# Two mixed pairs of single panels in another order, and a logarithm given out in three steps, in a one-layer hybrid inference step

## The chip, the cores and the metric

The kernel runs on one core of a Trainium2 chip. The metric is the device time of one execution in microseconds (us). Three runs of the kernel before took 1439.19, 1437.35 and 1439.19 us, median 1439.19.

## What is computed

One layer of a hybrid encoder, for 1024 prompt tokens and 64 sample tokens (T = 1088 rows, D = 1024), in float32. Cut to what matters here:

```python
xn = rms_norm(x, g_pre)
z = xn @ w_in
xa, ga, q, k, v, gb, fl, ma, mb = split(z)
logf = log_sigmoid(fl + b_f)
cum = cumsum(logf)
yb = fox_attend(q, k, v, cum, cum) * silu(gb)
log_a = -LRU_C * r * softplus(-a_param)
ya = rg_lru(causal_conv(xa), log_a) * silu(ga)
mix = sum(sigmoid([ma, mb]) * [ya @ w_a, yb @ w_b]) @ w_o
h = x + rms_norm(mix, g_post)
```

Both `log_sigmoid` and `softplus` go through one helper, `half_log1p_exp_neg_abs`: an exponential on ScalarE, and on VectorE a reciprocal and a series in seven coefficients. The keys, the values and `logf` are outputs too.

## The kernel before, in words

Every float32 product is made of three products of rounded halves: a high part (copied to fp32r by ScalarE, `copy_act`, L84) and the rest (subtracted by VectorE or GpSimd, `sub`, L87) of each operand, xh·wh, xh·wl and xl·wh. So each panel of weights that is loaded has to be split before TensorE can take it.

The stage of this change is the projection to keys, queries and some gates, from about 150 to 423 us of the span. It takes two panels of 128 columns at a time, a quad: `quads` (L224 to L230) lists twelve, numbered 0 to 11. Quads 0 to 7 are pairs of neighbouring panels of keys and queries by turns; quads 8 and 9 are mixed: two single panels each, out of the x path of branch A (`d_x0`, kind "r") and its gates (`d_ga`, kind "g"); 10 and 11 are pairs of merge or branch gates. `seven` (L852 on) makes a quad by seven products of halves, as in Strassen's scheme, with three PSUM banks (`ta`, `tb`, `tcc`), each used by two products or three. I call the n-th product of quad i qi.n. Each is 24 matmuls of 128x272 (`product`, L785 to L794). After q.1 ScalarE copies `ta` to `p1`, and q.3 adds on into `ta`, so it waits for that copy. After q.2 VectorE makes `u2` = `tb` + `p1` (L880), and q.4 adds on into `tb`, so it waits for `u2`. After q.4 VectorE makes `u3` (L897), and q.6 waits for that. The quarters of the result go through `put` (L817 on): a "k" or "q" quarter is split again (`oh` on ScalarE, `kl`, or for queries in place `ko`, on VectorE), and both parts are sent to DRAM, the `oh` by ScalarE's queue and the rest by SP's queue. A "g" quarter passes a Sigmoid on ScalarE (L827) and a product on VectorE (L828), an "r" quarter is sent as it is. `load_pair` (L623 on, its DMAs at L247) loads the panels of quad i + 2 at the start of quad i; `split_pair` splits those of quad i + 1 while quad i runs: GpSimd makes the four sums of panel halves (`s1`, `s2`, `s4`), ScalarE and VectorE the splits `wh` and `wl`.

Beside the quads runs a chain of small work, the generator `running_sums` (L700 to L767). `between`, called after every product, takes the chain one step on after every third product. Its steps, in this order:

- the forget gate's logarithm (`ls_e`, `ls_s`, `ls_q`, 128x144; the row of six at L158 is the series), `fl` (L710), `lf` (L711) and two DMAs that send `logf`;
- two steps with nothing in them;
- five matmuls for the cumulative sums (L720 to L724), and on VectorE `off` (L728 to L730) and `cs` (L732, L733);
- one step with nothing in it, and then eight steps, for each a transpose `ct` (L738), the six rows `cr` (L741 to L744, two of them casts on GpSimd) and a DMA to `d_rows`;
- two transposes `cs_t` (L748, L749), `cs_h` and `cs_n` (L753 to L755), and their DMAs;
- the softplus of the recurrence's parameter (`sp_e`, `sp_s`, `sp_q`, 128x8, with L764 to L767 behind it): seventeen instructions on VectorE and one exponential on ScalarE.

TensorE executes in the order in which the program is written. On ScalarE, VectorE, GpSimd and SP a scheduler sets the order in this stage, from the written order and its own costs; so a yield that is put into the chain doesn't by itself decide where the instructions behind it come to stand. A DMA takes one of eight lanes in turn and waits for the DMA that had its lane eight before.

Of the kernel before, what the change touches and what calls it, by code (L numbers as in the profile page):

```python
# [13 lines left out]
P = 128  # L14
D = 1024
KT = D // P
# [11 lines left out]
C_XA, C_GA, C_Q, C_K, C_V, C_GB, C_FL, C_MA, C_MB = (  # L28
    0, 1024, 2048, 3072, 4096, 5120, 6144, 6160, 7184)
# [20 lines left out]
GA_EARLY = (1, 3, 5)  # L50
LN1P = [1.0 / 15, 1.0 / 13, 1.0 / 11, 1.0 / 9, 1.0 / 7, 1.0 / 5, 1.0 / 3]
# [16 lines left out]
def hybrid_step(tc, a, o):  # L68
    nc = tc.nc
    PSUM = bass.MemoryType.PSUM  # L70
    act, dve, pool, pe, sp = nc.scalar, nc.vector, nc.gpsimd, nc.tensor, nc.sync

    def sb(name, bufs=1, side=None):
        kw = {"side": side} if side else {}
        return Pool(tc, name=name, bufs=bufs, reuse_waits="tile", **kw)
# [4 lines left out]
    def f(ap):  # L80
        return ap.bitcast(F32)

    def copy_act(out, in_, scale=1.0):
        return act.activation(out=out, in_=in_, func=AF.Copy, scale=scale)  # L84

    def sub(eng, out, in0, in1):
        return eng.tensor_tensor(out=out, in0=in0, in1=in1, op=ALU.subtract)  # L87
# [10 lines left out]
    d_ga = dram.tile([KT, P, T], F32, name="d_ga")  # L98
    d_x0 = dram.tile([P, T], F32, name="d_x0")
# [28 lines left out]
    def tiny(n, name, w=1, tag=None):  # L128
        return small.tile([P, w], F32, name=name, tag=tag or name)[:n, :]
# [17 lines left out]
    def half_log1p_exp_neg_abs(pl, x, w, name):  # L147

        e, s, q = (pl.tile([P, w], F32, name=f"{name}_{k}")[:, :] for k in "esq")
        tc.keep_in_program_order(dve.scalar_tensor_tensor(out=e, in0=x, scalar=-1.0, in1=x, op0=ALU.mult, op1=ALU.max))  # L150
        act.activation(out=e, in_=e, func=AF.Exp, scale=-1.0)
        dve.tensor_scalar(out=s, in0=e, scalar1=2.0, scalar2=None, op0=ALU.add)
        dve.reciprocal(out=s, in_=s)
        dve.tensor_tensor(out=s, in0=s, in1=e, op=ALU.mult)
        dve.tensor_tensor(out=q, in0=s, in1=s, op=ALU.mult)
        dve.tensor_scalar(out=e, in0=q, scalar1=LN1P[0], scalar2=None, op0=ALU.mult)
        for c in LN1P[1:]:
            dve.scalar_tensor_tensor(out=e, in0=e, scalar=c, in1=q, op0=ALU.add, op1=ALU.mult)  # L158
        dve.scalar_tensor_tensor(out=e, in0=e, scalar=1.0, in1=s, op0=ALU.add, op1=ALU.mult)
        return e  # L160
# [57 lines left out]
    def cols(c, n=2):  # L218
        return w_in[:, c:c + n * P]
# [2 lines left out]
                  for k in range(0, KT, 2))  # L222

    quads = [([cols(c + p * P)], ((t, p), (t, p + 1))) for p in range(0, NP, 2) for c, t in ((C_K, "k"), (C_Q, "q"))]  # L224
    some = [(cols(C_XA, 1), d_x0)] + [(cols(C_GA + k * P, 1), d_ga[k]) for k in GA_EARLY]
    for (s1, d1), (s2, d2) in (some[:2], some[2:]):
        quads.append(([s1, s2], (("r" if d1 is d_x0 else "g", d1), ("g", d2))))
    for _ in range(MORE):
        src, (d1, d2) = gates.pop()
        quads.append(([src], (("r", d1), ("r", d2))))  # L230
# [450 lines left out]
    p1b = sb("p1b")  # L681
# [18 lines left out]
    def running_sums():  # L700
        tri = p1b.tile([P, P], F32, name="tri")
        pool.memset(tri[:, :], 1.0)
        pool.affine_select(out=tri[:, :], in_=tri[:, :], compare_op=ALU.is_ge, fill=0.0,
                           base=0, pattern=[[1, P]], channel_multiplier=-1)
        nfl = (NBLK + 1) * NH
        fl2 = fl.rearrange("p b h -> p (b h)")
        hl = half_log1p_exp_neg_abs(p1b, fl2, nfl, "ls")
        lf = p1b.tile([P, NBLK + 1, NH], F32, name="lf")
        lf2 = lf.rearrange("p b h -> p (b h)")
        tc.keep_in_program_order(dve.tensor_scalar(out=fl2, in0=fl2, scalar1=0.0, scalar2=None, op0=ALU.min))  # L710
        dve.scalar_tensor_tensor(out=lf2, in0=hl, scalar=-2.0, in1=fl2, op0=ALU.mult, op1=ALU.add)  # L711
        sp.dma_start(o["logf_prompt"].rearrange("(b p) h -> p b h", p=P), lf[:, :NBLK, :])
        sp.dma_start(o["logf_sample"], lf[:DEC, NBLK, :])
        yield
        yield
        yield
        nb = NBLK * NH
        s_p = mm.tile([P, 512], F32, name="cum_p", tag="acc")
        cum_p, tot_p, cs_p, cs_p2 = s_p[:, :nb], s_p[:, nb:2 * nb], s_p[:, 2 * nb:2 * nb + NH], s_p[:, 2 * nb + NH:][:, :NH]
        pe.matmul(cum_p, tri[:, :], lf2[:, :nb], start=True, stop=True)  # L720
        pe.matmul(tot_p, ones[:, :P], lf2[:, :nb], start=True, stop=True)
        pe.matmul(cs_p, tri[:, :], lp[:, :], start=True, stop=True)
        pe.matmul(cs_p2[:DEC, :], ones[:, :DEC], lp[:, :], start=True, stop=False)
        pe.matmul(cs_p2[:DEC, :], tri[:DEC, :DEC], lf[:DEC, NBLK, :], start=False, stop=True)  # L724
        off = p1b.tile([P, NBLK, NH], F32, name="off")
        dve.memset(off[:, 0, :], 0.0)
        for b in range(1, NBLK):
            dve.tensor_tensor(out=off[:, b, :], in0=tot_p[:, (b - 1) * NH:b * NH], in1=off[:, b - 1, :], op=ALU.add)  # L728
        off2 = off.rearrange("p b h -> p (b h)")
        dve.tensor_tensor(out=off2, in0=cum_p, in1=off2, op=ALU.add)  # L730
        cs = p1b.tile([P, 2, NH], F32, name="cs")
        dve.tensor_copy(cs[:, 0, :], cs_p)  # L732
        dve.tensor_copy(cs[:DEC, 1, :], cs_p2[:DEC, :])  # L733
        yield
        yield
        for b in range(NBLK):
            ct = mm.tile([P, 512], F32, name="ct", tag="acc")[:NH, :P]
            pe.transpose(ct, off[:, b, :], ident[:, :])  # L738
            cr = p1b.tile([NH, 6, P], F32R, name="cr", tag="cr", bufs=1)
            copy_act(cr[:, 4, :], ct)  # L740
            sub(dve, cr[:, 5, :], ct, f(cr[:, 4, :]))  # L741
            dve.tensor_scalar(out=cr[:, 0:2, :], in0=f(cr[:, 4:6, :]), scalar1=-1.0, scalar2=None, op0=ALU.mult)
            for j in (2, 3):
                pool.tensor_copy(cr[:, j, :], ones[:NH, :P])  # L744
            sp.dma_start(d_rows[:, :, b * P:(b + 1) * P], f(cr[:, :, :]))
            yield
        cs_t = mm.tile([P, 512], F32, name="cs_t", tag="acc")
        pe.transpose(cs_t[:NH, :PAST], cs[:, 0, :], ident[:, :])  # L748
        pe.transpose(cs_t[:NH, PAST:PAST + DEC], cs[:DEC, 1, :], ident[:DEC, :DEC])  # L749
        cs_h = p1b.tile([NH, 2, PAST + DEC], F32R, name="cs_h")  # L750
        cs_n = p1b.tile([NH, 2, PAST + DEC], F32, name="cs_n")
        cs_t = cs_t[:NH, :PAST + DEC]
        copy_act(cs_h[:, 0, :], cs_t)  # L753
        sub(dve, cs_h[:, 1, :], cs_t, f(cs_h[:, 0, :]))
        dve.tensor_scalar(out=cs_n[:, :, :], in0=f(cs_h[:, :, :]), scalar1=-1.0, scalar2=None, op0=ALU.mult)  # L755
        sp.dma_start(d_cs, cs_n[:, :, :])
        sp.dma_start(d_cq.rearrange("s h t -> h s t"), f(cs_h[:, :, PAST:]))
        yield

        ap_ = vt[:, V_AP:V_AP + KT]  # L760
        hl2 = half_log1p_exp_neg_abs(p1b, ap_, KT, "sp")
        neg = p1b.tile([P, KT], F32, name="neg")
        tc.keep_in_program_order(
            dve.tensor_scalar(out=neg[:, :], in0=ap_, scalar1=-1.0, scalar2=0.0, op0=ALU.mult, op1=ALU.max))  # L764
        dve.scalar_tensor_tensor(out=neg[:, :], in0=hl2, scalar=2.0, in1=neg[:, :], op0=ALU.mult, op1=ALU.add)
        dve.tensor_scalar(out=sp4[:, :], in0=neg[:, :], scalar1=4.0, scalar2=None, op0=ALU.mult)
        dve.tensor_scalar(out=nsp8[:, :], in0=neg[:, :], scalar1=-8.0, scalar2=None, op0=ALU.mult)  # L767

    chain = running_sums()
    owed = deque()
    n_prod = [0]
# [1070 lines left out]
    for of in range(KT):  # L1845
        g = g_next
# [57 lines left out]
    for of in range(KT):  # L1904
        g, ma_ = m_next
# [244 lines left out]
    ss, r = tiny(n, "ss"), tiny(n, "r_r")  # L2150
    dve.tensor_reduce(out=ss, in_=ss4[:n, :], axis=AX.X, op=ALU.add)
    rstd_of(ss, r, 1.0 / D)
    for i in range(2):
        c = slice(i * D // 2, (i + 1) * D // 2)
# [52 lines left out]
```

## Time and profile before

| | |
|---|---|
| runs | 1439.19, 1437.35, 1439.19 us (median 1439.19) |
| the profiled execution | 1441.83 us; its span 1440.1 us |
| TensorE (PE) busy | 1417.7 us, 98% of the span |
| VectorE (DVE), ScalarE (ACT), GpSimd (POOL) | 851.2, 714.4, 276.9 us |
| chain that ended last | 89% PE, 5% DMA, 3% DVE, 1% ACT |

The span is one profiled execution; what lies around it (1.73 us here) is outside of its records. In the views, a row of a timeline begins with the start and the duration in us, and in brackets stands how long the engine was idle before it and what ended the wait. L793 is the matmul of the products of halves, L84 and L87 are the two helpers of the splits. SPq and ACTq rows are the issues of DMAs, not their transfers.

### The profile page before, as it was taken

What the parts mean: (1) busy time and instruction counts of PE and PEld (TensorE: products, weight loads), DVE (VectorE), ACT (ScalarE), POOL (GpSimd) and SP (SyncE); (2) the same over time, 40 slices, a digit from 0 to 9 for tenths busy, and PEclk for the clock granted to TensorE, in tenths of its full rate; (3) what the DMA queues carried; (4) which work ended last, traced back from release to release, by engine and by line L of the source; (5) the groups of instructions that cost most, each with busy time, mean ns of one, the idle gap of its engine ahead of it and who ended that gap; (6) DMA issues with size and microseconds to landing.
All of it is one profiled execution on the core that took longest, in us unless ns stands there. A gap on an engine that the chain in (4) does not pass through costs nothing.

```text
span 1440.1 us, 23751 instructions
## 1 busy us (share of the span) xinstructions
PE 1417.7 (98%) x8925; PEld 1352.0 (94%) x8925; DVE 851.2 (59%) x1495; ACT 714.4 (50%) x1297; POOL 276.9 (19%) x362
## 2 busy tenths in 40 slices
PE   8999999999999999999999999999999999999997
PEld 8999999989999999999999999999999999888886
DVE  5563855565524666565666657798755454337644
ACT  4423444334315666566666648878643322325543
POOL 0003324232313323333332320010023000000000
PEclk9999999999999999999999999999999999999999
DMA  5357456664368474545646354232296534224111
GB/s 204 115 131 106 133 156 189 140 173 137 84 174 218 127 154 127 143 122 147 132 117 154 61 95 58 45 57 47 102 299 212 188 126 151 74 70 166 48 48 45
DMA packets 134126, 182.68 MB, mean 127 GB/s; under 512 B 22276, under 2 KB 98604, under 8 KB 134012
## 3 DMA queue, kind: packets, MB, share of 16 engines
q1 hardware_dynamic: 116028, 154.90, 42.5%
q10 hardware_dynamic: 17680, 25.64, 5.0%
q8 instruction: 70, 1.15, 0.3%
q0 software_dynamic: 304, 0.62, 0.1%
q14 instruction: 44, 0.36, 0.1%
HBM read 122.65 MB, written 58.46 MB: 126 GB/s over the span
## 4 chain that ended last, share of the span: by engine, by line
PE 89%; DMA 5%; DVE 3%; ACT 1%; issue 1%; SPq 1%; ACTq 0%; DVEq 0%; POOL 0%; POOLq 0%
PE acc L165 16%; PE acc L166 16%; PE acc L167 16%; PE quad L793 15%; PE tp L1151 4%; PE pv L1179 2%; PE pv L1177 2%; PE s L1131 2%; PE s L1130 2%; PE vacc L458 1%; DMA w_raw<-in_w_in 1%; DMA d_q<-ko 1%; PE vacc L165 1%; DMA wf_raw<-in_w_in 1%; PE vacc L166 1%
## 5 line engine op out<-in xcount | busy, mean ns | idle before, releaser
L165 PE MATMUL acc<-xh,wh 128*128 128x368 f32 (+1 forms) x768 | 255.7, 333 | 0.0
L166 PE MATMUL acc<-xl,wh 128*128 128x368 f32 (+1 forms) x768 | 251.4, 327 | 0.0
L167 PE MATMUL acc<-xh,wl 128*128 128x368 f32 (+1 forms) x768 | 251.0, 327 | 0.0
L166 PEld LDWEIGHTS acc<-xl,wh 128*128 128x128 f32 x768 | 144.6, 188 | 3.1
L165 PEld LDWEIGHTS acc<-xh,wh 128*128 128x128 f32 x768 | 144.4, 188 | 3.0
L167 PEld LDWEIGHTS acc<-xh,wl 128*128 128x128 f32 x768 | 144.5, 188 | 0.0
L87 DVE TENSOR_TENSOR tl<-tp,th 128x512 fp32r<-128x512 f32 (+1 forms) x160 | 100.0, 633 | 57.9 <-ACT th L84 57.5
L84 ACT ACTIVATE th<-tp 128x512 fp32r<-128x512 f32 (+1 forms) x160 | 87.0, 552 | 66.4 <-PE tp L1151 59.7
L87 DVE TENSOR_TENSOR wl<-w_raw,wh 128x1024 fp32r<-128x1024 f32 (+1 forms) x65 | 74.1, 1140 | 58.6 <-ACT wh L84 49.5
L84 ACT ACTIVATE wh<-w_raw 128x1024 fp32r<-128x1024 f32 (+1 forms) x65 | 63.2, 974 | 72.5 <-PE acc L166 29.3
L1116 POOL TENSOR_SCALAR pb<-pb,sm 128x640 f32<-128x640 f32 (+1 forms) x64 | 61.8, 966 | 150.1 <-DVE sm L1115 150.1
L793 PE MATMUL quad<-xh,wh 128*128 128x272 f32 x384 | 81.9, 295 | 3.5 <-ACT p__3338 L84 3.5
L793 PE MATMUL quad<-xl,wh 128*128 128x272 f32 x384 | 80.5, 291 | 0.0
L793 PE MATMUL quad<-xh,wl 128*128 128x272 f32 x384 | 80.3, 291 | 0.0
L1113 ACT ACTIVATE pb<-pb,nm 128x640 f32<-128x640 f32 (+1 forms) x64 | 63.2, 987 | 25.3 <-DVE nm L1110 24.4
L1177 PE MATMUL pv<-tl,vv 128*128 128x512 f32 x192 | 74.4, 390 | 0.0
L1130 PE MATMUL s<-k,q 128*128 128x128 f32 (+2 forms) x192 | 66.9, 353 | 0.0
L1110 DVE CUSTOM_DVE_ANT_0 pb<-s,mask 128x640 f32<-128x640 f32 (+1 forms) x64 | 64.7, 1011 | 2.5 <-PE s L1131 2.2
L1131 PE MATMUL s<-k,q 68*128 68x128 f32 (+2 forms) x192 | 64.3, 347 | 1.5 <-DMA q<-d_rows 1.5
L793 PEld LDWEIGHTS quad<-xh,wh 128*128 128x128 f32 x384 | 61.2, 191 | 3.9 <-ACT p__3338 L84 3.7
L1151 PE MATMUL tp<-ident,pb 128*128 128x128 f32 x416 | 63.7, 272 | 0.0
L166 PE MATMUL acc<-ybl,wh 128*128 128x368 f32 (+1 forms) x192 | 62.9, 328 | 0.0
(538 smaller groups left out, 3748.8 us busy)
## 6 DMA issues: line engine op xcount, KB each, us to landing
w_raw<-in_w_in SPq DMA_DIRECT2D x60, 256.0 KB
q<-d_q SPq DMA_DIRECT2D x48, 256.0 KB
k<-d_k SPq DMA_DIRECT2D x48, 256.0 KB
w_raw<-in_w_branch SPq DMA_DIRECT2D x32, 256.0 KB
w_raw<-in_w_in SPq DMA_DIRECT2D x56, 128.0 KB
wraw<-in_w_in SPq DMA_DIRECT2D x20, 256.0 KB
d_k<-oh ACTq DMA_DIRECT2D x16, 272.0 KB
d_k<-kl SPq DMA_DIRECT2D x16, 272.0 KB
```

The source lines that it names most:

```text
L84: return act.activation(out=out, in_=in_, func=AF.Copy, scale=scale)
L87: return eng.tensor_tensor(out=out, in0=in0, in1=in1, op=ALU.subtract)
L165: pe.matmul(out, ah, bh, start=start, stop=False)
L166: pe.matmul(out, ah, bl, start=False, stop=False)
L167: pe.matmul(out, al, bh, start=False, stop=stop)
L793: pe.matmul(acc[:, c, :CW], l[:, k, :], r[:, k, c * CW:(c + 1) * CW], start=(first and k == 0 and p == 0), stop=(k == 3 and p == 2), skip_ ...
L1110: at = book("D", now[0] + HOP_PE, per(D_MAX, n), lambda: dve.tensor_tensor_reduce(out=pr[:, :n], in0=s[:, :n], in1=m, scale=-1.0, scalar=- ...
L1113: at = book("A", at, per(A_EXP, n), lambda: act.activation(out=pr[:, :n], in_=pr[:, :n], func=AF.Exp, scale=-1.0, bias=nm, accum_out=sm))
L1130: pe.matmul(s[:, c0:c0 + w], t["q1"][:, q], t["k1"][:, c0:c0 + w], start=True, stop=False)
L1131: pe.matmul(s[:, c0:c0 + w], t["q2"][:HD + 4, q], t["k2"][:HD + 4, c0:c0 + w], start=False, stop=True)
L1151: pe.transpose(tp[:, n:n + P], prs[u // 2, q][:, kb * P:(kb + 1) * P], ident[:, :])
L1177: pe.matmul(pv[:, 512 - n:], v, tl[:, c:c + n], start=(j == 0), stop=False)
```

## The change

It does two things.

First, the list of single panels is in another order. Before, quad 8 is (x panel 0, gate panel 1) and quad 9 (gate panel 3, gate panel 5). Now quad 8 is (gate 1, gate 3) and quad 9 (gate 5, x 0).

Second, `half_log1p_exp_neg_abs` becomes a generator with two yields, one after the first coefficient and one before the fourth. `running_sums` calls it twice, so all steps behind the first call come two steps, that is six products, later in the written order, and the end of the softplus twelve.

```diff
         dve.tensor_scalar(out=e, in0=q, scalar1=LN1P[0], scalar2=None, op0=ALU.mult)
-        for c in LN1P[1:]:
+        yield
+        for i, c in enumerate(LN1P[1:]):
+            if i == 3:
+                yield
             dve.scalar_tensor_tensor(out=e, in0=e, scalar=c, in1=q, op0=ALU.add, op1=ALU.mult)
...
-    some = [(cols(C_XA, 1), d_x0)] + [(cols(C_GA + k * P, 1), d_ga[k]) for k in GA_EARLY]
+    some = [(cols(C_GA + k * P, 1), ("g", d_ga[k])) for k in GA_EARLY] + [(cols(C_XA, 1), ("r", d_x0))]
     for (s1, d1), (s2, d2) in (some[:2], some[2:]):
-        quads.append(([s1, s2], (("r" if d1 is d_x0 else "g", d1), ("g", d2))))
+        quads.append(([s1, s2], (d1, d2)))
...
-        hl = half_log1p_exp_neg_abs(p1b, fl2, nfl, "ls")
+        hl = yield from half_log1p_exp_neg_abs(p1b, fl2, nfl, "ls")
...
-        hl2 = half_log1p_exp_neg_abs(p1b, ap_, KT, "sp")
+        hl2 = yield from half_log1p_exp_neg_abs(p1b, ap_, KT, "sp")
```

Three lines are added before L160, so in the rows of the changed program every line behind it has a number three higher (the six of L158 are now L161, `u2` is L883). No engine has an instruction more or fewer than before; they stand in other places. Three places matter.

**VectorE in quad 0**, from `u2` (u__1639) to `u3` (the second u_). Before:

```order
L880 TENSOR_TENSOR u__1639<-quad,p__1605 128x544
L158 SCALAR_TENSOR_TENSOR ls_e<-ls_e,ls_q 128x144 x6
L159 SCALAR_TENSOR_TENSOR ls_e<-ls_e,ls_s 128x144
L710 TENSOR_SCALAR fl<-fl 128x144
L87 TENSOR_TENSOR wl<-wraw,wh 128x1024
L711 SCALAR_TENSOR_TENSOR lf<-ls_e,fl 128x144
L839 SCALAR_TENSOR_TENSOR kl<-ko,oh 128x544
L897 TENSOR_TENSOR u__1731<-quad,p__1605 128x544
```

Now:

```order
L883 TENSOR_TENSOR u__1639<-quad,p__1605 128x544
L161 SCALAR_TENSOR_TENSOR ls_e<-ls_e,ls_q 128x144 x6
L162 SCALAR_TENSOR_TENSOR ls_e<-ls_e,ls_s 128x144
L713 TENSOR_SCALAR fl<-fl 128x144
L87 TENSOR_TENSOR wl<-wraw,wh 128x1024
L842 SCALAR_TENSOR_TENSOR kl<-ko,oh 128x544
L714 SCALAR_TENSOR_TENSOR lf<-ls_e,fl 128x144
L900 TENSOR_TENSOR u__1719<-quad,p__1605 128x544
```

The six of the series still stand in one row between `u2` and the splits; `lf` and `kl` have changed places, and all eight are still ahead of `u3`.

**ScalarE from the end of quad 5 to the start of quad 6**; p__3338 before and p__3319 now are `p1` of quad 6. Before:

```order
L84 ACTIVATE wh_3301<-s_3049 128x512
L84 ACTIVATE cs_h<-cs_t 16x192
L84 ACTIVATE oh<-ko 128x544
L837 DMA d_q<-oh 128x544
L84 ACTIVATE p__3338<-quad 128x544
L151 ACTIVATE sp_e<-sp_e 128x8
```

Now:

```order
L84 ACTIVATE wh_3282<-s_3031 128x512
L84 ACTIVATE cr<-ct 16x128
L84 ACTIVATE oh<-ko 128x544
L840 DMA d_q<-oh 128x544
L84 ACTIVATE p__3319<-quad 128x544
L84 ACTIVATE wh<-wraw 128x1024
```

In the place of `cs_h` stands a `cr`; `p1` stands behind `oh` and its DMA as before; the exponential of the softplus has gone to quad 7. The `cs_t` of TensorE has moved with `cs_h`, from behind q5.7 to behind q6.6, and the seventh and the eighth `ct` now stand behind q5.7 and q6.3.

**VectorE at the start of quad 7**; u__3667 before and u__3655 now are its `u2`. Before:

```order
L824 TENSOR_TENSOR ko<-quad,u__3372 128x544
L87 TENSOR_TENSOR wl_3579<-s_3342,wh_3578 128x512
L839 SCALAR_TENSOR_TENSOR kl<-ko,oh 128x544
L880 TENSOR_TENSOR u__3667<-quad,p__3627 128x544
L87 TENSOR_TENSOR wl<-w_raw,wh 128x1024
```

Now, from the third instruction of the softplus on (its first two, L150 and L152, stand just before these, behind the split of s_3323):

```order
L153 RECIPROCAL sp_s<-sp_s 128x8
L842 SCALAR_TENSOR_TENSOR kl<-ko,oh 128x544
L154 TENSOR_TENSOR sp_s<-sp_s,sp_e 128x8
L155 TENSOR_TENSOR sp_q<-sp_s 128x8
L156 TENSOR_SCALAR sp_e<-sp_q 128x8
L161 SCALAR_TENSOR_TENSOR sp_e<-sp_e,sp_q 128x8 x6
L162 SCALAR_TENSOR_TENSOR sp_e<-sp_e,sp_s 128x8
L767 TENSOR_SCALAR neg<-vt 128x8
L768 SCALAR_TENSOR_TENSOR neg<-sp_e,neg 128x8
L769 TENSOR_SCALAR sp_91<-neg 128x8
L770 TENSOR_SCALAR nsp_92<-neg 128x8
L883 TENSOR_TENSOR u__3655<-quad,p__3605 128x544
```

The whole softplus now stands in front of the `u2` of quad 7 (before: behind the `u2` of quad 6), and `cs_h` and `cs_n` stand a few instructions further ahead, among the last splits of quad 6.

## Rows read from the trace of the kernel before

**Rows 1.** The page: busy us of each engine (share of the span) and instructions.

```profile
PE 1417.7 (98%) x8925; PEld 1352.0 (94%) x8925; DVE 851.2 (59%) x1495; ACT 714.4 (50%) x1297; POOL 276.9 (19%) x362
```

**Rows 2.** Waits of PE, the second longest: us in total, times, longest us.

```profile
PE quad L793 <- ACT p__3338 L84: 3.5, 1, 3.5
```

**Rows 3.** Busy time by stretch: stretch, its length, engines, PEclk, DMA share, GB/s.

```profile
166.25:290.50 124.25, 123.57 (x990) 122.71 (x991) 71.61 (x106) 50.23 (x100) 39.90 (x34) 1.00 0.63 167
...
297.50:303.10 5.60, 5.59 (x24) 5.59 (x25) 3.89 (x19) 0.40 (x2) 1.33 (x1) 0.50 0.37 136
...
332.50:423.00 90.50, 90.50 (x723) 90.50 (x723) 45.55 (x55) 27.79 (x42) 25.30 (x28) 1.00 0.42 125
```

**Rows 4.** Timeline of PE at q6.3: start, us, engine, line, instruction, [idle before].

```profile
297.51 0.82 PE L793 MATMUL quad<-xh,wh 128*128 128x272 f32 x2 [3.47 <-ACT p__3338 L84]
298.13 0.66 PE L793 MATMUL quad<-xl,wh 128*128 128x272 f32 x2
```

**Rows 5.** Chain that ended last, from 256 to 300 us: start, us, what.

```profile
257.01 0.11 PE ct L738
...
277.92 11.97 DMA d_q<-ko
...
289.97 5.72 DMA d_q<-oh
...
295.78 0.67 ACT oh L84
...
296.84 0.63 ACT p__3338 L84
```

**Rows 6.** Timeline of DVE in quad 0, the series and `u3`.

```profile
157.63 5.45 DVE L158 SCALAR_TENSOR_TENSOR ls_e<-ls_e,ls_q 128x144 f32<-128x144 f32 x6
...
165.48 0.71 DVE L897 TENSOR_TENSOR u__1731<-quad,p__1605 128x544 f32<-128x544 f32 x1
```

**Rows 7.** Timeline of POOL in quad 0: first and last of four sums.

```profile
156.56 1.67 POOL L648 TENSOR_TENSOR s<-wraw 128x512 f32<-128x512 f32 x1 [12.47 <-DVE wl L87]
...
160.88 1.35 POOL L87 TENSOR_TENSOR s<-wraw,s 128x512 f32<-128x512 f32 x1
```

**Rows 8.** Timeline of PE at q0.6, behind q5.7, and at q7.3 and q7.4.

```profile
166.25 0.52 PE L793 MATMUL quad<-t4h,wh 128*128 128x272 f32 x2 [1.32 <-DVE u__1731 L897]
...
287.37 0.27 PE L748 MATMUL cs_t<-ident,cs 128*16 128x128 f32 x1
287.57 0.22 PE L749 MATMUL cs_t<-ident,cs 64*16 64x64 f32 x1
...
322.21 0.50 PE L793 MATMUL quad<-xh,wh 128*128 128x272 f32 x2
...
325.66 0.50 PE L793 MATMUL quad<-t3h,wh 128*128 128x272 f32 x2
```

**Rows 9.** Timeline of DVE in quads 6 and 7.

```profile
294.59 0.34 DVE L87 TENSOR_TENSOR cs_h<-cs_t,cs_h 16x192 fp32r<-16x192 f32 x1
...
295.63 1.42 DVE L755 TENSOR_SCALAR cs_n<-cs_h 16x384 f32<-16x384 f32 x1
...
300.18 1.17 DVE L158 SCALAR_TENSOR_TENSOR sp_e<-sp_e,sp_q 128x8 f32<-128x8 f32 x6
...
319.27 1.40 DVE L839 SCALAR_TENSOR_TENSOR kl<-ko,oh 128x544 f32<-128x544 f32 x1 [1.57 <-DMA d_k<-kl]
322.34 0.72 DVE L880 TENSOR_TENSOR u__3667<-quad,p__3627 128x544 f32<-128x544 f32 x1 [1.68 <-PE quad L793]
```

**Rows 10.** Timeline of ACT: `p1` of quad 7, and the table load of quad 8.

```profile
318.82 0.62 ACT L84 ACTIVATE p__3627<-quad 128x544 f32<-128x544 f32 x1 [1.51 <-PE quad L793]
...
351.67 1.28 ACT L827 ACT_TABLE_LOAD   x1
```

**Rows 11.** Timeline of POOL in quads 6 and 7: first and last of four sums.

```profile
313.73 1.67 POOL L648 TENSOR_TENSOR s<-w_raw 128x512 f32<-128x512 f32 x1 [14.90 <-DVE wl L87]
...
318.80 1.29 POOL L87 TENSOR_TENSOR s<-w_raw,s 128x512 f32<-128x512 f32 x1
```

## The prediction

> **What bounds the kernel now.** I read the busy times first. TensorE is busy for 1417.7 us [rows 1] of a span of 1440.1, so all that any change can win without taking work from TensorE is the 22.4 us in which it stands idle, and what it loses at a lower clock. Next come its waits, for the stage that the change touches. The longest wait for ScalarE or VectorE inside the quads is one of 3.5 us, for `p1` of quad 6 [rows 2]. The timeline shows it at q6.3, 3.47 us of idle time, and the pairs of matmuls behind it take 0.66 us each [rows 4]. The stretches say why: the 24 matmuls of q6.3 take 5.60 us at a granted clock of 0.50, that is at 1.2 of 2.4 GHz, where the stretch before ran 990 matmuls in 123.57 us at 1.00, so 3.00 us for 24 [rows 3]. So this one stop costs 3.47 + 2.60 = **6.07 us**. What TensorE did before its clock fell was to stand idle for 3.47 us. The second stop in the stage is 1.32 us at q0.6, for `u3` of quad 0 [rows 8]; the stretch that begins there ran at 1.00 [rows 3], so it cost nothing more. From 332.5 to 423 us TensorE is busy for 90.50 of 90.50 us [rows 3]: in quads 8 and 9, where the panels change places, there is nothing to win.
>
> Then the chain says what lies behind the two stops. At q6.3 it goes back over `p1` on ScalarE, an `oh` that stands ahead of it in ScalarE's queue, and two transfers of query quarters: one of 5.72 us from 289.97, one of 11.97 us from 277.92 [rows 5]. It is a stop by DMA. At q0.6 VectorE is late: its row of six for the logarithm takes 5.45 us, and `u3` follows only at 165.48 [rows 6]. GpSimd's four sums run from 156.56 to 162.23 [rows 7], so the six, some 0.9 us each, stand beside them almost for their whole length. For six instructions of the softplus, a smaller tile, the row without a sum beside it takes 1.17 us [rows 9].
>
> **The change part by part.** I make the sum against the profiled execution, 1441.83 us (span 1440.1). The median of the runs is 2.64 us lower, 1439.19; I take the difference of the sum from that.
>
> *The logarithm in quad 0: 0.* The text puts yields into the series, but the order of VectorE shows its six instructions in one row between `u2` and the splits, as before, and the same eight ahead of `u3`; only `lf` and `kl` have changed places. So the stop of 1.32 us stays. The ends: if the three steps came apart, −1.32; nothing is added ahead of `u3`, so at most nothing on the other side.
>
> *The cumulative sums in quad 2 in place of quad 1, and eight transposes six products later: −0.2 and +0.1.* The work is the same. VectorE is busy for 71.6 of 124.25 us there and TensorE for 123.57 [rows 3], so the place costs nothing. But at q6.3 all waits for a chain that TensorE leaves at about 274 us; what stands on TensorE before that time counts, what stands between it and the stop is hidden, and what stands behind counts again. Two `ct`, 0.11 us each [rows 5], leave the part before 274 (−0.22), one comes into the hidden part and one behind the stop (+0.11).
>
> *`cs_t` from in front of the stop to behind it: +0.4.* Its two transposes run from 287.37 to 287.79 [rows 8], in hidden time, and will run behind q6.6 in open time: +0.42.
>
> *The stop at q6.3: 0.* It keeps its chain. The last `oh` of quad 5 and its DMA still stand ahead of `p1`, and a `cr` of the same small size takes the place of `cs_h`. Of the transfers that go out between 274 and 295 us, none is added or taken away: the two DMAs of `cs` that leave went out about 295 us or later, behind the 5.72 us transfer, and a `d_rows` takes their place. The ends are wide, since these transfers are priced by what else is under way: −6.07 if the stop goes, and +6.25 if the second transfer takes 11.97 us like the first in place of 5.72 [rows 5].
>
> *The softplus and `cs` ahead of `u2` of quad 7: 0, with little to spare.* Seventeen instructions at 1.17 / 6 = 0.195 us are 3.3 us; `cs_h` and `cs_n` are 0.34 + 1.42 us [rows 9]. All of it now stands on VectorE ahead of `u2` of quad 7. Before, that part of VectorE had 1.57 us idle ahead of `kl` and 1.68 ahead of `u2` [rows 9]; `u2` ended at 323.06, and q7.4, which waits for it, began at 325.66 [rows 8], so 2.60 more. That makes 5.85 us of cover for 5.1 us. By the order: `cs_h` and `cs_n` stand ahead of a `kl` whose transfer the next `kl` waits for, so that one, at 319.27, comes 1.76 later and ends at 322.43; three instructions of the softplus lie in its wait, fourteen behind it, 2.73 us, to 325.16; `u2`, 0.72, to 325.88. Due is 325.66 + 0.53 for the `ct` and `cs_t` that TensorE now has in between, 326.19. So 0.3 us are left. `p1` on ScalarE now has the softplus's exponential ahead of it, which waits for VectorE; it ended at 319.44 [rows 10] and is due at 322.21 [rows 8], which leaves 2.77. The ends: below zero nothing, as no stop is there to be won; above, see the second rival. What is queued behind: the exponential holds up a `d_k` transfer and `p1`, and the softplus holds up `u2` and the split of quad 8's panels behind it, which isn't due before q8.1.
>
> *The panels of quads 8 and 9: 0.* Both quads load the same two single panels' worth, and quad 8 now has four Sigmoid quarters and quad 9 two, for two and four. The table load, 1.28 us [rows 10], comes a product earlier. Quad 9 had four such quarters before, inside the 90.50 of 90.50 busy us [rows 3], so that number of quarters is covered by rows; the load and its Sigmoid are some 1.9 us on ScalarE, which is idle for 62.7 of those 90.5 us. The ends: 0, and +1.28 if the load stood on the path whole.
>
> The sum is −0.22 + 0.11 + 0.42 = **+0.3 us**: 1442.1 against the profiled 1441.83, or 1439.5 against the median. What a measurement of this kernel can tell from no change is about 0.2%, 2.9 us, so the forecast is no change that can be told.
>
> **The rivals.**
>
> *A, the logarithm does come apart*, and `u3` of quad 0 comes in time: −1.32 + 0.3, **1438.2**. For it speaks the text of the change, against it the order of VectorE. It would still read as no change.
>
> *B, the stop at q6.3 goes or shrinks.* It rests on two transfers, 11.97 and 5.72 us [rows 5], in a stretch where the transfers stand in each other's way, and three small ones (`cs`, `logf`, `d_rows`) have other neighbours now; the second of them took half the time of the first, so some microseconds are loose here. If `p1` comes 3.47 us sooner, all of it goes, with the half clock: −6.07 + 0.3, **1433.4**. If it comes 2.2 sooner, a stop of 1.3 is left, which at q0.6 brought no lower clock, and −4.8 + 0.3 gives 1434.7. Against it speaks that the transfers which set it, and their predecessors, are the same.
>
> *C, `u2` of quad 7 comes late: slower.* In quad 0 a row of six small instructions on VectorE took 5.45 us beside GpSimd's sums [rows 6, 7]. In quad 7 the four sums run from 313.73 to 320.09 [rows 11], and the softplus begins just behind them; GpSimd now has two more casts for a `cr` in front of these sums. If they come later so that two of them lie beside the fourteen instructions, these take two sums of 1.67 us more. C decides from the point where `u2` ends behind 326.2, 0.3 us away: 3.34 − 0.3 = 3.0 us of stop, and, if that is long enough for the half clock as 3.47 was, 2.6 on top: +3.3 to +5.9, in the middle **1443.8**. One sum alone gives +1.7, which doesn't read as slower. The Trainium skill speaks for this rival: "SBUF — State Buffer", section "SBUF: two separate sides", has VectorE and GpSimd share a pair of ports as a lock that is held for a whole instruction, for a VectorE instruction with two SBUF inputs among others. By that rule, each such instruction of the softplus that meets a sum waits to its end; the trace agrees in quad 0, where the six took 5.45 us. Against C speaks the reckoning above, by which the sums are over before the fourteen begin.
>
> *D, the stop at q6.3 grows*, by the same loose transfers as B: from a microsecond up to +6.25, say +3.5 + 0.3, **1443.0**.
>
> **How the numbers follow.** Forecast, with up to one sum in quad 7: 0.58. A: 0.06. B: 0.20, because the largest price in the stage hangs on transfers that I can bound only loosely. C: 0.10. D: 0.06. B is faster by over 0.2%, 0.20; the forecast and A are within it, 0.64; C and D slower, 0.16. The predicted time is the forecast's, 1439.5. Its own range is 1437.3 (the lowest run before, or A) to 1441.5 (one sum met, and a little). To hold 8 in 10 the range reaches down to B, 1433.4, and leaves C and D, 0.16, outside beyond 1442.0.
>
> **What would show it.** Right: PE still idle for about 1.3 us ahead of q0.6 with the six still 5 us and more; about 3.5 us ahead of q6.3, for `p1`, with a clock of 0.50 behind it; no idle time ahead of q7.3 and q7.4, with `u2` ending about 325.9 less the shift of the whole; and 332.5 to 423 full. Wrong: a wait of q7.4 for `u2` of quad 7 (C); a q6.3 that starts without a wait (B) or with one of 5 us or more (D); the six of the logarithm in three pieces (A). The forecast is wrong as a whole if the time moves by over 2.9 us.

## The result and the profile after

The changed kernel takes 1444.58 us (median of 6, 1443.45 to 1445.88), the kernel before in the same runs 1439.38 (1437.35 to 1441.20): a ratio of 1.0037, 95% interval 1.0026 to 1.0047. It is **slower by about 5 us**, where I forecast no change that can be told and a range that ended at 1442.0. The profiled execution took 1445.88 us. Medians, here and below, are of all runs of a kernel, and the ratios aren't their quotients and leave out two runs at a far lower granted clock (1659.34 us of the changed kernel with other columns, whose median without it is 1435.12, and 2334.72 us of the kernel before).

The waits of TensorE after, longest first (us in total, times, longest us), in the place of [rows 2]:

```profile
PE tpk L807 <- ACT st L84: 5.5, 1, 5.5
PE vacc L461 <- ACT wvh L84: 3.7, 1, 3.7
PE quad L796 <- DVE u__3739 L900: 2.0, 1, 2.0
PE s L1134 <- DMA q<-d_rows: 1.6, 1, 1.6
PE wake L444 <- POOL ident L113: 1.6, 1, 1.6
PE quad L796 <- DVE u__1719 L900: 1.3, 1, 1.3
```

The wait for `p1` of quad 6 is not in the list: the stop at q6.3 is gone. The 1.3 us at q0.6 are still there (u__1719). New are 5.5 us for a `tpk`, the transposed keys, and 2.0 us for u__3739, the `u3` of quad 7. The stretches after (length, then busy us and instructions of PE, PEld, DVE, ACT, POOL, then PEclk, DMA share, GB/s), beside [rows 3]:

```profile
290.50:325.94 35.44, 35.44 (x286) 35.09 (x285) 22.15 (x43) 12.03 (x23) 11.94 (x9) 1.00 0.62 130
325.94:334.46 8.52, 1.04 (x7) 0.37 (x5) 1.42 (x3) 2.93 (x6) 0.00 (x0) 0.79 0.53 109
334.46:340.07 5.61, 5.61 (x33) 5.61 (x34) 3.35 (x6) 2.71 (x8) 0.00 (x0) 0.71 0.84 210
```

From 290.5 to 325.94, over the place where the stop was, TensorE is full. Then it works 1.04 us of 8.52, and what follows begins at the lower clock. The timeline of TensorE shows the two waits and the end of the slow part:

```profile
331.86 0.64 PE L807 MATMUL tpk<-ident,ko 128*64 128x128 f32 x2 [5.51 <-ACT st L84]
334.46 0.82 PE L796 MATMUL quad<-t4h,wh 128*128 128x272 f32 x2 [1.96 <-DVE u__3739 L900]
...
336.89 0.66 PE L796 MATMUL quad<-t4h,wl 128*128 128x272 f32 x2
...
338.02 0.41 PE L796 MATMUL quad<-t4h,wl 128*128 128x272 f32 x2
```

The 24 matmuls of q7.6 run from 334.46 to 339.02, 4.56 us in place of some 3.0. So the new stop costs about 5.5 + 2.0 + 1.5 = **9.0 us**, the one before 6.07. The chain that ended last says for what (start, us, what):

```profile
318.17 13.17 DMA out_k_prompt<-st
...
331.42 0.38 ACT st L84
331.81 0.53 ACT ko L84
...
332.35 0.67 ACT oh L84
...
333.04 0.73 DVE ko L842
333.77 0.65 DVE u__3739 L900
```

A transfer of transposed keys to the output, 128 KB, took 13.17 us. It is the last of two that held up ScalarE, which puts a piece of the keys into one of three buffers (one `kst`, two `st`) before it is sent:

```profile
329.87 0.38 ACT L84 ACTIVATE kst<-tpk 128x256 f32<-128x256 f32 x1 [9.59 <-DMA out_k_prompt<-kst]
331.42 0.38 ACT L84 ACTIVATE st<-tpk 128x256 f32<-128x256 f32 x1 [1.17 <-DMA out_k_prompt<-st]
```

TensorE can't use the PSUM bank of `tpk` until ScalarE has emptied it; and in ScalarE's queue behind `st` stand the `ko` and `oh` on which VectorE's queue, and so `u3`, wait. The DMA of that time, 318 to 326 us, after and then before:

```profile
DMA packets 712, 0.35 MB, mean 43 GB/s; under 512 B 38, under 2 KB 712, under 8 KB 712
```

```profile
DMA packets 2520, 1.91 MB, mean 238 GB/s; under 512 B 210, under 2 KB 2248, under 8 KB 2520
```

With the DMA engines busy in both (about 1.00 and 0.94 of their time), 43 GB/s went through in place of 238. The same view of the kernel before, from 282 to 290 us, where the 11.97 us transfer of [rows 5] is under way:

```profile
DMA packets 789, 0.61 MB, mean 77 GB/s; under 512 B 57, under 2 KB 646, under 8 KB 789
```

So a slow time of the DMA engines has moved, from quad 6 to quad 7. What moved with it is the load of one single panel. From the semaphores of the DMA lanes, the landing times (us) of the four 128 KB transfers of each single panel, in the two traces:

```
panel (first column)   before                          after
x 0     (0)            282.4  286.5  289.1  291.7      321.4  324.2  327.2  329.2
gate 1  (1152)         292.6  294.7  298.1  298.6      280.2  283.3  285.3  286.3
gate 3  (1408)         317.1  318.1  320.2  321.8      287.4  287.9  291.7  292.6
gate 5  (1664)         322.2  324.9  325.6  326.0      312.5  313.0  315.5  315.6
```

The pieces of x 0 land 2 to 4 us apart in both, one after the other, with little else beside them. From the first issue to the last landing x 0 took 15.3 us before (from 276.41) and 13.9 after (from 315.29), gates 3 and 5 before 7.4 each. So x 0 goes out in quad 5 before, though its load is written at the start of quad 6, and in quad 7 after. The 512-byte packets took 194 ns each on average from 283 to 289 us before and 192 ns from 318.5 to 326 after, against 41 ns for those of gate 5 from 311 to 315.3.

### The profile page after: what moved, and what is told of

The parts are those of the page before. It is cut to its first block, busy times and chain, and to the rows that moved or that the text cites. A ratio compares the mean times of both kernels' runs of the same rounds, so it can differ in the third digit from the quotient of the medians.

```text
span 1444.2 us, 23750 instructions
## 1 busy us (share of the span) xinstructions
PE 1418.0 (98%) x8925; PEld 1351.4 (94%) x8925; DVE 851.3 (59%) x1495; ACT 714.0 (49%) x1297; POOL 275.2 (19%) x362
## 4 chain that ended last, share of the span: by engine, by line
PE 89%; DMA 5%; DVE 3%; ACT 1%; SPq 1%; issue 0%; ACTq 0%; DVEq 0%
PE acc L168 16%; PE acc L169 16%; PE acc L170 16%; PE quad L796 16%; PE tp L1154 4%; PE pv L1182 2%; PE pv L1180 2%; PE s L1134 2%; PE s L1133 2%; PE vacc L461 1%; DMA w_raw<-in_w_in 1%; DMA out_k_prompt<-st 1%; DMA wf_raw<-in_w_in 1%; PE vacc L168 1%; PE vacc L169 1%; PE vacc L170 1%
## 5 line engine op out<-in xcount | busy, mean ns | idle before, releaser
L1182 PE MATMUL pv<-th,vv 128*128 128x512 f32 x192 | 62.9, 345 | 0.0
```

Source lines behind the costliest of these rows:

```text
L1182: tc.declare_no_dep(pe.matmul(pv[:, 512 - n:], v, th[:, c:c + n], start=False, stop=(j == last and i == len(parts) - 1)).ins, high.ins, re ...
```

## The experiments

Theory S: the x path's first panel is slow to load in itself, and costs what stands behind it in the DMA engines; so its place sets the time. Theory Y: the yields do it, with `cs` and the softplus at the end of quad 6. Theory P: any single panel is slow in that place. Times are medians; "before" is the kernel before on the same chip.

| run | us | before | ratio, 95% interval |
|---|---|---|---|
| order of panels alone | 1442.85 | 1438.85 | 1.0031 [1.0020, 1.0042] |
| yields alone | 1439.17 | 1438.85 | 1.0007 [0.9997, 1.0016] |
| before, other columns for x 0 | 1434.02 | 1438.85 | 0.9965 [0.9953, 0.9978] |
| after, other columns for x 0 | 1435.71 | 1438.85 | 0.9974 [0.9963, 0.9985] |
| x 0 in the last quad | 1435.81 | 1438.68 | 0.9985 [0.9976, 0.9994] |
| the same, with the yields | 1437.70 | 1438.68 | 0.9989 [0.9980, 0.9999] |
| after, x 0 from GpSimd's queue | 1438.52 | 1438.68 | 1.0005 [0.9994, 1.0015] |
| before, slow columns for gate 5 | 1442.35 | 1438.45 | 1.0026 [1.0017, 1.0035] |
| x 0 in the last quad, chain later | 1435.02 | 1438.45 | 0.9986 [0.9976, 0.9996] |

**The order of the panels alone.** The kernel before with the hunk of `some` and `quads.append` of the diff, and no yield.

> The kernel before with the new order of the single panels alone (quad 8: gates 1 and 3; quad 9: gate 5 and x 0), the logarithm undivided. Theory S: the x path's first panel (columns 0 to 127 of w_in) is itself slow to load. Its four transfers of 128 KB landed 3 to 4 us apart in the kernel before (282.4, 286.5, 289.1, 291.7 us) and 2 to 3 us apart in the changed kernel (321.4, 324.2, 327.2, 329.2), where the gates' panels land about 1 to 2 us apart; whatever is sent behind it waits, in quad 6 before and in quad 7 now. Then the order alone gives all of the change: 1443 to 1446 us, no stop at q6.3, and a stop of 5 us or more in quad 7 with transfers of the keys' output behind the x panel. Rival Y: the yields do it, because the softplus and the DMAs of cs stand at the end of quad 6 now; then the order alone gives 1433 to 1440 us.

Measured: 1442.85 us, 4.0 over the kernel before, under S's lower end by a little. The waits of TensorE:

```profile
PE tpk L804 <- ACT st L84: 4.1, 1, 4.1
...
PE quad L793 <- DVE u__3751 L897: 2.2, 1, 2.2
```

The same two waits as in the changed kernel, the first 4.1 us instead of 5.5, and none at q6.3. Y falls: the order alone gives most of the change.

**The yields alone.** The kernel before with the other hunks.

> The kernel before with the two yields in the logarithm alone, the panels in the order of before. Theory S (the slow x panel): the stop of about 3.5 us at q6.3 and the half clock behind it stay, quad 7 has no stop, 1438.5 to 1440.5 us. Rival Y (the yields): a stop of several us in quad 7, 1443 to 1446 us, or on top of the stop at q6.3 1447 and more.

Measured: 1439.17 us, at 1.0007 of before not to be told from it. In quad 7 there was no stop; at q6.2 and at q6.3 TensorE waited 1.06 and 1.58 us with no lower clock, where the profile of before has one stop of 3.47 and I had expected it to stay:

```profile
285.00:300.00 15.00, 12.36 (x97) 11.87 (x97) 8.09 (x11) 5.12 (x10) 7.25 (x7) 1.00 0.90 205
```

One profile can't tell whether the yields made the stop smaller. But it is not the same in each execution of the same instructions: in the profile of the probe below, which is the kernel before up to its end, it is 2.71 us, with a granted clock of 0.89 from 290 to 305 us, against 3.47 us and 0.77 in the profile of before (1441.83 us, near the top of its runs).

**Other columns for x 0.** One term more in the line of `some`, here for the order of before, and the same in the changed kernel's line; it computes the x path of the first 128 channels from other weights:

```diff
-    some = [(cols(C_XA, 1), d_x0)] + ...
+    some = [(cols(C_XA + P, 1), d_x0)] + ...
```

> The kernel before, but the x path's first panel is read from columns 128 to 255 of w_in in place of 0 to 127 (so the x path of the first 128 channels is computed from other weights; sizes, order and instructions are the same). Theory S (the slowness goes with these columns): the four transfers land 1 to 2 us apart, the stop at q6.3 is gone or under 1 us, no half clock, 1432.5 to 1435 us. Rival P (any single panel of 512-byte pieces is slow in this place, whichever columns it takes): the stop stays, 1438.5 to 1440.5 us.

> The changed kernel, but the x path's first panel is read from columns 128 to 255 of w_in in place of 0 to 127 (as in the run before this, other weights for the first 128 channels of the x path). Theory S: the stop in quad 7 goes, 1432.5 to 1436 us. Rival P or Y: it stays, 1443 to 1446 us.

Measured: 1434.02 us for the order of before, 1435.71 for that of the changed kernel. With the same instructions in the same order, only another address, 4.8 us of the one and 8.9 us of the other are gone (the second against the 1444.58 of the first section, where the kernel before was at 1439.38). The stretches of the first, and then the waits of the second:

```profile
290.50:303.10 12.60, 12.60 (x103) 12.60 (x102) 11.56 (x29) 4.88 (x8) 5.33 (x3) 1.00 0.50 139
303.10:332.50 29.40, 29.40 (x239) 29.36 (x238) 17.30 (x21) 13.17 (x26) 7.59 (x5) 1.00 0.67 193
```

```profile
PE quad L796 <- DVE u__1719 L900: 1.3, 1, 1.3
PE quad L796 <- DVE u__3739 L900: 1.0, 1, 1.0
```

No stop and no lower clock in quads 6 and 7 of the first; 1.0 us for `u3` of quad 7 in the second. P falls.

**The slow panel in quad 7, with the order of before.** The reverse test: x 0 from quick columns, and gate 5, the last of quad 9, from columns 2048 to 2175 (`C_Q` in place of `C_GA + 5 * P`).

> The kernel before, its order and all its instructions as they are, with two panels read from other columns: the x path's first panel from 128 to 255 (quick to load) and gate 5, the last single panel of quad 9, from 2048 to 2175 (slow: 13.6 us for 512 KB in the probe). So the first 128 channels of the x path and the panel of gate 5 are computed from other weights. Theory S: only the place of the slow panel makes the difference between the two kernels: no stop at q6.3, a stop of 4 to 6 us in quad 7 for the keys' output behind the panel and one of about 2 us for u3, 1441.5 to 1445 us, as with the new order alone (1442.9). Rival: what is multiplied and sent in which quad also counts (kinds and their stores); then it stays at 1433 to 1437 us.

Measured: 1442.35 us. The waits of TensorE, in a profile of 1439.24 us, the lowest of the ten runs; none is at q6.3:

```profile
PE tpk L804 <- ACT st L84: 3.6, 1, 3.6
...
PE quad L793 <- DVE u__3751 L897: 2.0, 1, 2.0
```

The two waits of the changed kernel appear in a program whose instructions stand as in the kernel before; the first is 0.4 us below what I expected. So it's the place of a slow panel, not what is multiplied or sent where.

**Panels by themselves.** At the end of the kernel before, twenty panels loaded one after the other, each into the same buffer, beside what is left of the kernel's own work:

```diff
+    for c in (0, 128, 0, 16, 64, 512, ...):
+        load_panel(p7.tile([P, KT, P], F32, name="probe", bufs=1)[:, :, :], cols(c, 1))
```

> The kernel before, and at its end twenty single panels loaded one after the other into one buffer that nothing reads, from the columns 0, 128, 0, 16, 64, 512, 896, 1024, 1152, 2048, 2176, 3072, 4096, 5120, 5248, 6144, 6160, 7168, 7184 and 256. Theory S1 (panels that begin at a multiple of 1024 columns, 4096 bytes, are slow, and every time): 0 both times, 1024, 2048, 3072, 4096, 5120, 6144 and 7168 take 10 us and more each for 512 KB, the others 4 to 7 us. Rival S2 (the first reading of a panel is slow, later ones not): 0 is fast at the end, since it was read before. Rival S3 (only the neighbourhood in time made it slow): all panels alike.

Measured, from first issue to last landing of the 512 KB, from the trace:

```
first column   us            first column   us
0              15.4, 13.4    128            10.2
16             13.9          256             8.5
64             10.4          512             7.7
1024           13.4          896             8.5
2048           13.6          1152            8.0
3072           13.3          2176            8.2
4096           14.2          5248            7.8
5120           13.6
6144, 6160     13.7, 13.7
7168, 7184     13.6, 13.3
```

S1 holds, though with three things that I had not expected: panels that begin 16 columns behind a multiple of 1024 are as slow, the quick ones take 7.7 to 10.2 us and not 4 to 7, and the one 64 behind takes 10.4. That last one is not slow in the same way: its 1024 packets took 35 ns each on average and the DMA engines were busy for 0.28 of its time, where the second load of column 0 had 166 ns and 0.81. The 10.2 us of column 128 came beside other transfers (173 GB/s in all). They are slow each time they are read, so S2 falls. In the traces of the kernel itself gate 0 (column 1024) has it too: its pieces landed at 827.3, 830.8, 833.7 and 836.0 us, where no stop came of it.

**The panel from another queue.** The changed kernel, with the four transfers of x 0 issued by GpSimd:

```diff
-            load_panel(dst, s)
+            load_panel(dst, s, queue=pool if i == 9 and s is src[-1] else sp)
```

> The changed kernel, with the four transfers of the x path's first panel issued by GpSimd instead of SP, all else as it is. Theory Q (the keys' output waits because it stands behind the panel in SP's queue): the outputs of keys in quad 7 land within 2 to 5 us of their issue though the panel itself still takes 10 us or more, the stop in quad 7 shrinks to under 2 us, 1434 to 1438 us. Theory E (the panel holds all 16 DMA engines, whoever issues it): the outputs still take 8 us and more, the stop stays, 1442 to 1446 us.

Measured: 1438.52 us, 6 under the changed kernel. The chain and the waits of TensorE:

```profile
313.12 11.79 DMA out_k_prompt<-st
```

```profile
PE quad L796 <- DVE u__3739 L900: 2.2, 1, 2.2
...
PE tpk L807 <- ACT st L84: 0.8, 1, 0.8
```

Each theory got one half. By E's account, the transfers still took long: 9.4 to 11.8 us for the four that SP issued beside the panel, so another queue doesn't get past it. Q's time was nearly right, and by the traces for another reason: SP did not have the panel to issue, so the output that waits longest went out 0.9 us behind the last `d_k` transfer of quad 6 (312.21 to 313.12), in the changed kernel 3.3 us behind it (314.91 to 318.17). It landed 6.4 us earlier, 1.7 of which the whole program stood earlier in this profile (`cs_t` at 304.11 against 305.83). The stop shrank to 0.8 + 2.2 us, and the clock stayed at 1.00 behind it. The Trainium skill has the first half of this ("DMA: Bandwidth & Descriptors", section "Issuing engines are not separate DMA queues"): transfers of all issuing engines run on the same 16 DMA engines. The trace agrees with its 11.79 us.

**x 0 where little waits behind it.** The mixed pair of gate 5 and x 0 becomes quad 11, behind the two pairs of gates, without yields and with them:

```diff
-    for (s1, d1), (s2, d2) in (some[:2], some[2:]):
-        quads.append(([s1, s2], (d1, d2)))
+    mixed = [([s1, s2], (d1, d2)) for (s1, d1), (s2, d2) in (some[:2], some[2:])]
+    quads.append(mixed[0])
     for _ in range(MORE):
...
+    quads.append(mixed[1])
```

> The kernel before (no yields) with the mixed pair that holds the x path's first panel moved to the last quad (quad 8: gates 1 and 3; 9 and 10: the two pairs of gates; 11: gate 5 and x 0), so that its slow load goes out in quad 9, from about 355 us, where quad 8 gives out gates alone and hardly anything is sent behind it. Theory S (the slow panel costs what waits behind it): no stop at q6.3 and none in quad 7, TensorE full from 290 to 423 us, 1432.5 to 1436 us. Rival: the load is as late for quad 11 as it was for the others, a stop of several us in quad 10 or 11, 1438 to 1444 us.

> The same place of the x path's first panel, with the two yields in the logarithm as in the changed kernel. If the yields are worth nothing by themselves (they gave +0.07% [-0.03, +0.16] alone), the same as the run before this within 2 us, 1432.5 to 1437 us. If the softplus and cs ahead of u2 of quad 7 cost something once the stop at q6.3 is gone, a wait of q7.4 for u2, and 2 to 4 us more than the run before.

Measured: 1435.81 and 1437.70 us. In the first, x 0 took 14.0 us to load, from 353.7 to 367.7, and TensorE did not stop:

```profile
290.50:332.50 42.00, 42.00 (x339) 41.96 (x339) 27.50 (x48) 18.05 (x34) 11.91 (x9) 1.00 0.57 168
332.50:423.00 90.50, 90.50 (x707) 90.50 (x707) 38.97 (x48) 24.38 (x37) 21.41 (x26) 1.00 0.48 117
353.00:368.00 15.00, 15.00 (x122) 15.00 (x121) 7.26 (x8) 3.96 (x6) 3.81 (x3) 1.00 0.96 112
```

It beats both kernels, though not by all that the columns gave (1434.02); its profile has 2.2 us of waits at the start of the attention, for its first keys and rows, and whether the panel's place brought them isn't settled. The yields gave no gain here; the two intervals overlap, and q7.4 did not wait for `u2`. The 1437.70 us are a little above the range for yields that are worth nothing. Their profile has a wait of 2.76 us for the rows at the start of the attention, at 453.91 us, and a granted clock of 0.76 from 455 to 462 us; without the yields it is 1.29 us and 1.00.

**The logarithm behind u3.** The same, with `chain_at = [6]` in place of `[3]`.

> The x path's first panel in the last quad, as in the run of that place, no yields, and the chain of small work begun three products later (its first step behind q0.6 in place of q0.3), so that the logarithm stands on VectorE behind the two splits and u3 of quad 0, not ahead of it. If the stop of 1.3 us at q0.6 is the logarithm's place beside GpSimd's sums, it goes, no other comes in its place, and the time is about 1.3 us under the run with the panel alone (1435.8): 1433 to 1436 us. Rival: the logarithm, wherever it stands, holds up the next u2 or u3 (in quad 1), and the time stays at 1435 to 1437.5 us with a stop of 1 us or more in quad 1.

Measured: 1435.02 us; the ratio to before, 0.9986, is not to be told from that of the run without it, 0.9985. The stop at q0.6 is gone, as the first stretch shows, and none comes in quad 1:

```profile
149.50:166.25 16.75, 16.75 (x137) 16.75 (x135) 10.58 (x13) 8.09 (x13) 5.45 (x4) 1.00 0.39 108
166.25:300.00 133.75, 133.75 (x1075) 132.98 (x1074) 87.23 (x132) 58.18 (x112) 45.45 (x38) 1.00 0.61 177
```

So it is shown that the logarithm's place ahead of `u3` makes that stop (how much of it GpSimd's sums add, this run doesn't separate), and its worth in the time is not: one wait behind it, for the rows at the start of the attention, was 2.24 us, and 1.29 in the run without it.

## Why the prediction was wrong

**What failed is the step on the panels of quads 8 and 9: "Both quads load the same two single panels' worth".** They are the same in bytes and not in time: x 0 took 15.3 and 13.9 us to load in the two traces, gates 3 and 5 before 7.4. I counted transfers, and the change exchanged a slow load for a quick one at the end of quad 5 and in quad 6, and the reverse in quad 7. The term that I put at 0, with +1.28 as its upper end, measured +4.0 us when the order was changed alone. The step on the stop at q6.3 fell with it: "Of the transfers that go out between 274 and 295 us, none is added or taken away". In number none was, but x 0's four left this place and a gate's came. Three of the four went out ahead of the 11.97 us transfer of [rows 5], the last right behind it, and the transfer landed 0.8 us after the third. A look at the landing times of the loads one by one, 3 us apart for one panel and about 1 for another, would have shown it before; the chain names only the transfer that waits, and I took its length for the general press of transfers.

**The rivals.** B came, at a chance of 0.20: the stop at q6.3 went, with the half clock. But B was priced alone, and its price came back larger in quad 7, in no rival's place. C priced a late `u2` of quad 7; it was `u3`, and not for the softplus. The time I gave for C (1443.8) is near the measured one by chance.

**What held.** The logarithm in quad 0 stayed in one row, and the stop is 1.27 us, against 1.32 before [rows 8]. The softplus ahead of `u2` of quad 7 cost nothing:

```profile
310.58 1.26 DVE L150 SCALAR_TENSOR_TENSOR sp_e<-vt 128x8 f32<-128x8 f32 x1
...
315.39 1.18 DVE L161 SCALAR_TENSOR_TENSOR sp_e<-sp_e,sp_q 128x8 f32<-128x8 f32 x6
...
317.24 0.72 DVE L883 TENSOR_TENSOR u__3655<-quad,p__3605 128x544 f32<-128x544 f32 x1
```

GpSimd's sums met its first instruction (1.26 us for one) and not the six. `u2` ended at 317.96, and q7.4 began at 319.63 with no wait, 1.7 us to spare where I had reckoned 0.3. And the yields as a whole, +0.3 us by the sum, measured +0.07% [-0.03, +0.16], that is about 1 us and not to be told from nothing.

**Where the 5 us come from.** In the profiles, 6.07 us of stop went and about 9.0 came, and the span grew by 4.1; the other 1.2 us I haven't traced. In the medians, the columns took 4.8 us off before and 8.9 off after: the same slow panel costs about 4 us more in quad 7 than in quad 6. Two things speak for why, and no run tests either by itself. First, the stop in quad 6 seems not to come in full each time: nearly all runs of the kernel before have mean granted clocks between 0.993 and 0.998, where its profile, with the stop, has 0.994 and the profile of x 0 in the last quad, without it, 0.997. The six runs of the changed kernel all have 0.993 or 0.994. Second, before, only three pieces of the transposed keys were still to be sent when x 0 went out; two went out behind it and took 13.0 and 12.8 us, and TensorE did not stop for them, but for `p1`, by way of a query quarter in ScalarE's queue. After, eight were still to come, for three buffers, and their lateness reached TensorE's PSUM bank and `u3`.

## What to carry to other kernels

When work is moved, don't take equal bytes for equal transfers: read the landing times of each load that changes place, not only those on the chain. A slow transfer costs what is behind it in the DMA engines, so it belongs where nothing that is needed soon goes out behind it; another issuing queue doesn't get past it, though here it won back 6 of the 8.9 us. And a stop that leaves one place is priced to the end only when one has asked where its cause goes.

## What was not expected of the hardware

Panels of 128 columns of a matrix of 8208 float32 columns load in 13.3 to 15.4 us per 512 KB when they begin at a multiple of 1024 columns (4096 bytes) or 16 columns behind it, and in 7.7 to 10.2 at 128 and more; the number of packets (1024) and their size (512 bytes) are the same. The one at 64 behind took 10.4, with packets of 35 ns and DMA engines that were busy for 0.28 of the time. The rows lie 32832 bytes apart, so each row's piece begins 64 bytes further into a stretch of 4096 bytes than the one above it, and over 64 rows the pieces of any panel go through all such places. The first column's place in 4096 bytes thus doesn't by itself say why some panels suffer; that stays open. The Trainium skill tells of a like effect ("DMA: Bandwidth & Descriptors", section "Latency and other measured facts"): copies are slower at row pitches of large powers of two, from 2 MiB on. No run here shows whether it is the same; the pitch here is far smaller, and the first column decides.

In the quads, TensorE's granted clock fell to 0.50 with a stop of 3.47 us in the kernel before, of 5.51 in the changed one and of 2.71 in the profile of the probe; with waits of 0.8 and 2.2 us close together (the panel from GpSimd's queue) and of 1.06 and 1.58 (the yields alone) it stayed at 1.00. But the length of one wait doesn't decide it. At the start of the attention the clock from 455 to 462 us is 0.76 behind a wait of 1.64 us (the yields alone) and of 1.57 (the panel from GpSimd's queue), and 1.00 behind 2.24 (the chain later). What decides it no run here separates.
